# State space heads with outputs by channels, a first loop ordered by the scheduler, and an attention whose third and fourth queries are projected earlier

## The chip, the cores and the metric

The kernel runs on one core of a Trainium2 chip. The metric is the device time of one execution in microseconds (us); lower is better. Engines: TensorE (PE: matmuls, with weight loads in a queue of their own, PEld), VectorE (DVE), ScalarE (ACT), GpSimd (POOL), and SyncE (SP), which issues the DMAs of weights.

## The reference

One layer of a hybrid decoder on 256 tokens, D = 2048, in float32. Cut to what matters here:

```python
a = rmsnorm(h, attn_norm_g)
z, xBC, dt, q, k, v = split(a @ w_in)
x, B, C = silu(causal_conv4(xBC))              # x: 32 heads of 64; B, C: 4 groups of 128
# per group g (8 heads), chunks c of 128 tokens, acs = cumsum(dt * A):
y[l]  = sum_{s<=l} (C[l].B[s]) * exp(acs[l]-acs[s]) * dt[s]*x[s]      # own chunk
y[l] += exp(acs[l]) * C[l] @ prev_state                                # chunk before
y     = (y + d_skip * x) * silu(z)
y_ssm = rmsnorm_per_group(y) * ssm_norm_g
# attention: per-head norm of q and k, partial rope, window of 128, a sink per head
y_att = softmax_with_sink(q @ k.T) @ v
h = h + concat(y_ssm, y_att) @ w_out
h = h + w_down(silu(g) * u),  [g | u] = causal_conv3(rmsnorm(h) @ w_up)
h = h + sigmoid(rmsnorm(h) @ w_pg) * rmsnorm(p @ w_pe)
```

## The kernel before

The 256 tokens are two blocks b of 128. A float32 product is made of three matmuls: both factors are split into a high part in TensorE's fast float32 form and a low part (the rest), and hi·hi, hi·lo and lo·hi are added up in PSUM (lines 222 to 224 in `products`). A weight tile w is 128 x 2 x 512 (two k of 128 rows for 512 columns, 512 KB); it comes by DMA (line 207), ACT casts it to wh (line 192), DVE subtracts to wl (line 193), and it feeds 12 matmuls: 2 k, 2 blocks, 3 products. Pools: seven tiles w (`WR`), four each of wh and wl (`WB`), two pairs of accumulators acc, two tr tiles for transposes and two ms tiles in PSUM.

Stages in order, as far as the change goes:

*The first loop* (lines 340 to 379) projects the chunks B and C. Its weight tiles hold one k for the two chunks, so there are 16 tiles and two accumulator pairs, acc_b and acc_c. The order of PE's instructions is the code's (`manual_schedule`, line 339): per k first all six matmuls of chunk B, then those of C. Of the first three k each half of the tile is cast and subtracted by itself. Ahead stand 13 warm-up matmuls on constants (line 155). The dt products (lines 335 and 336) are spread over k = 11 to 13 and the end. Then `evac_scaled` (line 389) copies the accumulators to SBUF, ACT copies the dt sums to hsq (line 427), and chunks B and C are transposed and convolved (lines 299, 286, 288).

*The state space (SSD) stage* has four groups g; from here to the attention a scheduler orders the instructions of each engine. `ssd_x(g)` projects x (96 matmuls), loads the row differences seg from DRAM, makes the decays (seg, 128 x 8 x 128 per chunk, lines 484 to 497), convolves x and transposes it back to tokens (line 516); from that come the skip term yc (line 518) and Xd = dt·x (line 521). The heads: per chunk eight matmuls with seg as weights and Xd as moving data (64 columns, line 534), added to yc (line 535); for chunk 1 also the product with the state prev (line 538), scaled by exp(acs) on DVE (line 541) and added (line 542). So y has tokens on the partitions. `ssd_gate(g)` projects z (96 matmuls) and takes its Silu. `ssd_end` multiplies (line 557), sums squares on ACT, takes rstd (`rstd`, with a power on POOL, line 187), scales (line 561), transposes y on PE (line 272) and splits it (lines 195, 196) into the left factor of the output projection. Output 0 is projected here, outputs 1 to 7 (1 to 3 of the SSD, 4 to 7 of the attention) later.

*The attention* again has PE's order written by hand, in slots of 12 matmuls (2.7 us): keys 0 to 7, queries 0 8 to 15, values 16 to 23, queries 1 24 to 31, output 1 32 to 39, queries 2 40 to 47, output 2 48 to 55, queries 3 56 to 63, then outputs 3 to 7. A table `at` says ahead of which slot the scores (three pieces) and the value products of head pair j stand. Queries are normed and rotated, written as 16-bit halves by POOL (`half`), transposed by a DMA that SP issues in its order among the weight loads (line 688), and put together by POOL (line 689) to qT, for which the scores (line 738) wait. Scores go to DVE (s, line 742; nm, line 749), and the value products (line 779) run in pairs, with 64 weight columns each, into the two halves of the partitions. `add_to_h` (line 396) adds a projection to the residual h. Feed-forward and the rest are not touched.

Of the kernel before, what the change touches and what calls it, by code (L numbers as in the profile page):

```python
# [20 lines left out]
P = 128  # L21
# [44 lines left out]
def hybrid_layer(  # L66
# [87 lines left out]
    for _ in range(13):  # L154
        PE.matmul(ps, lhsT=one[:, :P], rhs=one, start=True, stop=True)
# [162 lines left out]
    with xin_:  # L318
        wd = sb(xin, [P, KT, 32], "wd")
        dhl = sb(xin, [P, KT, 64], "dhl", F32R)  # L320
        parts = {}

        def first_products(k, c):

            wh, wl = parts[k]
            acc = (acc_b, acc_c)[c]
            for part, wt in enumerate((wh, wh, wl)):
                for b in range(NB):
                    PE.matmul(acc[b], lhsT=aT(k, b)[part % 2], rhs=wt[:, c, :], start=(k == 0 and not part), stop=(k == KT - 1 and part == 2))

        dt_ps = ms_tile()

        def dt_products(k):
            hi, lo = aT.part(k)
            PE.matmul(dt_ps[:64, :T], lhsT=dhl[:, k, :], rhs=hi, start=(k == 0), stop=False, skip_group_check=True)
            PE.matmul(dt_ps[:32, :T], lhsT=dhl[:, k, :32], rhs=lo, start=False, stop=(k == KT - 1), skip_group_check=True)

        by_hand = ExitStack()
        by_hand.enter_context(tc.manual_schedule(engines={PE.engine}))
        for k in range(KT):  # L340
# [9 lines left out]
            n = 1 if k < 3 else KW  # L350
            for c in range(0, KW, n):
                split(w[:, c : c + n, :], wh[:, c : c + n, :], wl[:, c : c + n, :])
            parts[k] = wh, wl
            if k < KT - 2:
                for c in range(KW):
                    first_products(k, c)
            if k == 8:
                nc.sync.dma_start(wd, w_dt)
                nc.sync.dma_start(scw, ssm_cw)
                nc.sync.dma_start(rw, rows.partition_broadcast(P))  # L360
                nc.sync.dma_start(posi, pos)
                split(wd, dhl[:, :, :32], dhl[:, :, 32:])
# [5 lines left out]
            if k in (11, 12, 13):  # L368
                for i in range(4 * k - 44, 4 * k - 40):
                    dt_products(i)  # L370
        for c in range(KW):
            for k in (KT - 2, KT - 1):
                first_products(k, c)
        for k in range(KT - 4, KT):
            dt_products(k)
        by_hand.close()
        rx_ = rstd(ssx, D, NB, "rx_")
        V.tensor_copy(rx, rx_)

# [13 lines left out]
    def add_to_h(acc, n):  # L393
        for b in range(NB):
            hs = hres[b][:, n * NC : (n + 1) * NC]
            V.tensor_tensor(out=hs, in0=hs, in1=acc[b], op=ALU.add)  # L396
# [13 lines left out]
    def project(lhs, w, i0, ni, after=None):  # L410

        for n in range(4):
            acc = acc_pair()
            gemm(acc, lhs, [w[i, n] for i in range(i0 * KG // KW, (i0 + ni) * KG // KW)])
            add_to_h(acc, n)
# [5 lines left out]
    with tc.tile_pool(name="ssd", bufs=1) as sp, tc.tile_pool(name="dram", bufs=1, space=bass.MemoryType.DRAM) as dp:  # L421
        BT = sb(sp, [P, 4, T], "BT")
        CT = sb(sp, [P, 4, T], "CT")
        for c, (acc, dst, tag) in enumerate(((acc_b, BT, "ct"), (acc_c, CT, "Xd"))):
            t = evac_scaled(acc, sp, tag, 1)
            if c == 0:
                S.copy(dtT, dt_ps[:64, :T])
# [45 lines left out]
        eacs = sb(sp, [P, 64], "eacs")  # L473
        S.activation(out=eacs, in_=acs, func=AF.Exp)

        def ssd_x(g):
            segs = []
            for c in range(NB):
# [3 lines left out]
                if c == 0:  # L482
                    dec = sb(sp, [P, 8], "dec", bufs=2)
                    V.tensor_tensor(out=dec, in0=seg[:, :, P - 1], in1=acs[:, hs], op=ALU.subtract)
                    S.activation(out=dec, in_=dec, func=AF.Exp)
                V.tensor_tensor(out=seg, in0=seg, in1=bc(acs[:, hs], P), op=ALU.subtract)
# [25 lines left out]
            y, Xd = [], []  # L512
            for b in range(NB):
# [15 lines left out]
            for c in range(NB):  # L529
                yc = y[c]  # L530
                yp = ms_tile()
                for h in range(8):
                    hs = slice(h * HD, (h + 1) * HD)
                    PE.matmul(yp[:, hs], lhsT=segs[c][:, h, :], rhs=Xd[c][:, hs], start=True, stop=True)
                V.tensor_tensor(out=yc, in0=yc, in1=yp, op=ALU.add)
                if c:
                    off = ms_tile()
                    PE.matmul(off, lhsT=CT[:, g, c * P : (c + 1) * P], rhs=prev, start=True, stop=True)
                    t = sb(sp, [P, NC], "xe")
                    o = g * 16 + 8  # L540
                    V.tensor_tensor(out=v3(t, 8), in0=v3(off, 8), in1=bc(eacs[:, o : o + 8], HD), op=ALU.mult)
                    V.tensor_tensor(out=yc, in0=yc, in1=t, op=ALU.add)
# [11 lines left out]
        def ssd_end(g, y, zs):  # L554
            ssy = sb(sp, [P, NB], "ssy", bufs=2)
            for b in range(NB):
                V.tensor_tensor(out=y[b], in0=y[b], in1=zs[b], op=ALU.mult)
                S.activation(out=zs[b], in_=y[b], func=AF.Square, accum_out=ssy[:, b : b + 1])
            ry = rstd(ssy, NC, NB, "ry")
# [441 lines left out]
```

## Time and profile before

| | |
|---|---|
| Time, median of 3 runs | 1432.73 us (1432.59 to 1434.25) |
| The profiled execution | 1436.61 us, of which the span is 1434.9 us |
| Granted clock of TensorE | 1.00 |
| HBM | read 268.32 MB, written 2.13 MB |
| First loop | up to 55.11 us (the first transposes behind it) |
| SSD stage | about 55 to 316 us (last transposes of y at 315.33) |
| Scores of the attention, first wait for qT | 371.95 us |

Durations of single instructions come from the profiled execution; they are read against its span, not against the median. A matmul row shows the time from issue to its modelled end, so that neighbours overlap: the distance of two starts is what one costs. In the timeline and the groups below, "x16" counts instructions, and a plain float32 product shows as two.

### The profile page before, as it was taken

How to read it: one execution, taken by the hardware profiler on the slowest of the kernel's cores; microseconds unless marked ns; L12 is line 12 of the kernel's file. 1: busy time of each engine (PE TensorE's matmuls, PEld its weight loads, DVE VectorE, ACT ScalarE, POOL GpSimd, SP SyncE). 2: the span in 40 equal slices, each digit the busy share in tenths (PEclk: the TensorE clock that was granted, in tenths of full speed). 3: DMA queues.
4: the chain of work that ended last, by engine and by line, in shares of the span. 5: the costliest groups of instructions: out<-in, count | busy, mean ns of one | idle time of the engine just before them, and what ended most of it. 6: DMA issues, size and time to landing. Idle time of an engine off the chain costs nothing.

```text
span 1434.9 us, 18092 instructions
## 1 busy us (share of the span) xinstructions
PE 1423.2 (99%) x6527; PEld 1167.3 (81%) x6527; DVE 984.1 (69%) x1242; ACT 804.2 (56%) x1101; POOL 286.2 (20%) x212
## 2 busy tenths in 40 slices
PE   9999999999999999999999999999999999999998
PEld 7887888888787778888888888888888888888887
DVE  6678876776678897656667646765675576476854
ACT  6675555644567666556556446545554554455643
POOL 0002010008345432013243112201320131120000
PEclk9999999999999999999999999999999999999999
DMA  9656656548687778577887767867876877776671
GB/s 332 236 173 198 215 177 185 171 148 223 188 220 187 209 220 220 168 211 207 219 226 202 217 205 206 225 196 198 230 208 192 223 201 218 206 208 190 208 226 65
DMA packets 163467, 292.62 MB, mean 204 GB/s; under 512 B 93041, under 2 KB 95921, under 8 KB 162993
## 3 DMA queue, kind: packets, MB, share of 16 engines
q1 hardware_dynamic: 162944, 290.99, 70.5%
q8 instruction: 51, 0.84, 0.2%
q10 hardware_dynamic: 432, 0.48, 0.1%
q14 instruction: 40, 0.32, 0.1%
HBM read 268.32 MB, written 2.13 MB: 188 GB/s over the span
## 4 chain that ended last, share of the span: by engine, by line
PE 68%; DVE 1%; ACT 0%; issue 0%; POOL 0%; DVEq 0%; ACTq 0%
PE acc L222 22%; PE acc L224 22%; PE acc L223 22%; PE tr L779 1%; PE tr L272 0%; PE sc L738 0%; DVE wl L193 0%; ACT s L753 0%; DVE nm L749 0%; DVE s L742 0%; ACT wh L192 0%; DVE sg L931 0%; ACT s L761 0%; DVE qkr L672 0%; DVE h L396 0%
## 5 line engine op out<-in xcount | busy, mean ns | idle before, releaser
L193 DVE TENSOR_TENSOR wl<-w,wh 128x1024 fp32r<-128x1024 f32 (+1 forms) x495 | 634.9, 1288 | 378.5 <-ACT wh L192 376.4
L192 ACT CAST wh<-w 128x1024 fp32r<-128x1024 f32 (+1 forms) x495 | 514.8, 1045 | 480.7 <-PE acc L224 431.4
L223 PE MATMUL acc<-wl,ah 128*128 128x512 f32 x1278 | 500.1, 391 | 1.5 <-DVE wl L193 1.5
L224 PE MATMUL acc<-wh,al 128*128 128x512 f32 x1278 | 499.0, 391 | 0.0
L222 PE MATMUL acc<-wh,ah 128*128 128x512 f32 x1278 | 498.3, 392 | 0.0
L223 PEld LDWEIGHTS acc<-wl,ah 128*128 128x128 f32 x1278 | 240.1, 188 | 52.3 <-DVE wl L193 2.4
L222 PEld LDWEIGHTS acc<-wh,ah 128*128 128x128 f32 x1278 | 240.1, 188 | 51.0 <-issue 1.4
L224 PEld LDWEIGHTS acc<-wh,al 128*128 128x128 f32 x1278 | 240.1, 188 | 50.1 <-issue 0.7
L224 PE MATMUL acc<-wh,gl 128*128 128x512 f32 x352 | 137.1, 390 | 0.0
L223 PE MATMUL acc<-wl,gh 128*128 128x512 f32 x352 | 137.1, 390 | 0.0
L222 PE MATMUL acc<-wh,gh 128*128 128x512 f32 x352 | 136.5, 390 | 0.0
L881 POOL COPY half<-u 128x1024 uint16<-128x1024 uint16 x44 | 62.0, 1422 | 264.3 <-ACT u L879 264.3
L222 PE MATMUL acc<-wh,yh 128*128 128x512 f32 x256 | 101.6, 397 | 0.6 <-DVE h L396 0.6
L223 PE MATMUL acc<-wl,yh 128*128 128x512 f32 x256 | 99.9, 390 | 0.0
L224 PE MATMUL acc<-wh,yl 128*128 128x512 f32 x256 | 99.7, 390 | 0.0
L884 POOL COPY uc<-flip 128x1024 uint16<-128x1024 uint16 x44 | 54.9, 1248 | 177.2 <-DMA flip<-half 174.9
L223 PEld LDWEIGHTS acc<-wl,gh 128*128 128x128 f32 x352 | 66.1, 188 | 13.7
L224 PEld LDWEIGHTS acc<-wh,gl 128*128 128x128 f32 x352 | 66.1, 188 | 13.6
L222 PEld LDWEIGHTS acc<-wh,gh 128*128 128x128 f32 x352 | 66.1, 188 | 13.6
L288 DVE SCALAR_TENSOR_TENSOR cv<-uc,fcw,cv 128x254 f32<-128x254 f32 (+1 forms) x176 | 73.2, 476 | 3.4 <-ACT cv L286 3.4
L396 DVE TENSOR_TENSOR h<-h,acc 128x512 f32<-128x512 f32 x112 | 73.0, 678 | 1.8 <-PE acc L224 1.8
L222 PEld LDWEIGHTS acc<-wh,yh 128*128 128x128 f32 x256 | 48.1, 188 | 14.6 <-issue 2.0
(239 smaller groups left out, 1129.2 us busy)
## 6 DMA issues: line engine op xcount, KB each, us to landing
w<-in_w_up_dram SPq DMA_DIRECT2D x176, 512.0 KB, 4.2
w<-in_w_in_dram SPq DMA_DIRECT2D x126, 512.0 KB, 4.2
w<-in_w_down_dram SPq DMA_DIRECT2D x88, 512.0 KB, 4.3
w<-in_w_out_dram SPq DMA_DIRECT2D x64, 512.0 KB, 4.2
w<-in_w_pg_dram SPq DMA_DIRECT2D x32, 512.0 KB, 4.3
seg<-scr SPq DMA_DIRECT2D x8, 512.0 KB, 5.0
xt<-in_xT_dram SPq DMA_DIRECT2D x16, 128.0 KB, 7.0
h<-in_x_dram SPq DMA_DIRECT2D x2, 1024.0 KB, 8.7
```

Of the source, the lines that this page charges most:

```text
L192: S.copy(hi, src)
L193: V.tensor_tensor(out=lo, in0=src, in1=hi.bitcast(F32), op=ALU.subtract)
L222: PE.matmul(acc[b], lhsT=hi, rhs=wh[:, i, :], start=(k == 0), stop=False)
L223: PE.matmul(acc[b], lhsT=hi, rhs=wl[:, i, :], start=False, stop=False)
L224: PE.matmul(acc[b], lhsT=lo, rhs=wh[:, i, :], start=False, stop=(k == total - 1 or (b == NB - 1 and k + 1 == whole)))
L288: V.scalar_tensor_tensor(out=dst[:, s:], in0=ps[:, : T - s], scalar=taps[n - 1 - s], in1=dst[:, s:], op0=ALU.mult, op1=ALU.add)
L396: V.tensor_tensor(out=hs, in0=hs, in1=acc[b], op=ALU.add)
L779: PE.matmul(v3(o[e * HD : (e + 1) * HD, kv * 2 * P : (kv + 1) * 2 * P], 2), lhsT=v[kb][:, vs], rhs=pT[e][:, :, kb, :], start=(kb == 0), st ...
L881: G.tensor_copy(half.rearrange("p (a n) -> p a n", a=2), u_.bitcast(U16).rearrange("p (n a) -> p a n", a=2))
L884: G.tensor_copy(uc[:, :, b * P : (b + 1) * P].bitcast(U16).rearrange("p f (t a) -> p f t a", a=2), flip.rearrange("p (a f) t -> p f t a", ...
```

## The change

1. **First loop.** Eight warm-up matmuls instead of 13. PE's order is the scheduler's. Only k = 0 is split in halves. The small loads for dt come after k = 3 instead of 8. The dt products use one ms tile after the loop in the code, and ACT's copy of them stands directly behind.
2. **SSD heads.** y has channels on the partitions, 128 x 4 x 256. The state term goes into the same accumulation: a tile grown = exp(acs)·C for chunk 1, made by ACT and DVE, is the moving factor and prev the weight. Two heads write the two halves of the partitions. The skip is added while y is read from PSUM. z is brought to channels by POOL copies (16-bit halves), a DMA transpose that SP issues, and POOL copies back (zT), as the queries are. The split reads y directly, with no transpose on PE. The squares are summed over channels by a reduction and two matmuls with a column of ones, and rstd is applied when the output projection is added to h.
3. **Attention.** Order: queries 1, queries 2, output 1, queries 3, output 2, outputs 3 to 7. The table of scores and values is shifted.

```diff
-    for _ in range(13):
+    for _ in range(8):
         PE.matmul(ps, lhsT=one[:, :P], rhs=one, start=True, stop=True)
...
-        by_hand.enter_context(tc.manual_schedule(engines={PE.engine}))
...
-            n = 1 if k < 3 else KW
-            for c in range(0, KW, n):
-                split(w[:, c : c + n, :], wh[:, c : c + n, :], wl[:, c : c + n, :])
-            parts[k] = wh, wl
-            if k < KT - 2:
-                for c in range(KW):
-                    first_products(k, c)
-            if k == 8:
+            for c in range(0, KW, 1 if k == 0 else KW):
+                cs = slice(c, c + 1 if k == 0 else KW)
+                split(w[:, cs, :], wh[:, cs, :], wl[:, cs, :])
+            for c, acc in enumerate((acc_b, acc_c)):
+                for b in range(NB):
+                    h, l = aT(k, b)
+                    PE.matmul(acc[b], lhsT=h, rhs=wh[:, c, :], start=(k == 0), stop=False)
+                    PE.matmul(acc[b], lhsT=h, rhs=wl[:, c, :], start=False, stop=False)
+                    PE.matmul(acc[b], lhsT=l, rhs=wh[:, c, :], start=False, stop=(k == KT - 1))
+            if k == 3:
...
+        S.copy(dtT, ps[:64, :T])
...
-    def add_to_h(acc, n):
+    def add_to_h(acc, n, scale=None):
...
+                V.scalar_tensor_tensor(out=hs, in0=acc[b], scalar=scale[:, b : b + 1], in1=hs, op0=ALU.mult, op1=ALU.add)
...
+                else:
+                    grown = sb(sp, [P, 8, P], "grown")
+                    S.activation(out=grown, in_=seg, func=AF.Exp)
+                    V.tensor_tensor(
+                        out=grown, in0=grown, in1=CT[:, g, P:].unsqueeze(1).to_broadcast([P, 8, P]), op=ALU.mult
+                    )
...
-                yc = sb(sp, [P, NC], f"yc{b}", bufs=2)
-                V.tensor_tensor(out=v3(yc, 8), in0=v3(tr, 8), in1=bc(dsk[:, g * 8 : (g + 1) * 8], HD), op=ALU.mult)
-                y.append(yc)
...
-                    PE.matmul(yp[:, hs], lhsT=segs[c][:, h, :], rhs=Xd[c][:, hs], start=True, stop=True)
-                V.tensor_tensor(out=yc, in0=yc, in1=yp, op=ALU.add)
-                if c:
-                    off = ms_tile()
-                    PE.matmul(off, lhsT=CT[:, g, c * P : (c + 1) * P], rhs=prev, start=True, stop=True)
...
+                own = [(0, i, Xd[0], segs[0]) for i in range(2)]
+                for i in range(2):
+                    own += [(1, i, Xd[1], segs[1]), (1, i, prev, grown)]
+                for c, i, left, right in own:
+                    for e_ in range(2):
+                        h = 4 * half + 2 * i + e_
+                        PE.matmul(
+                            yp[e_ * HD : (e_ + 1) * HD, i, c * P : (c + 1) * P],
+                            lhsT=left[:, h * HD : (h + 1) * HD],
+                            rhs=right[:, h, :],
...
+                    V.scalar_tensor_tensor(
+                        out=y[:, f, :], in0=xc[:, f, :], scalar=skip[:, 4 * g + f : 4 * g + f + 1], in1=yp[:, i, :], op0=ALU.mult, op1=ALU.add
+                    )
...
+                half = sb(sp, [P, 2 * NC], ("xe", "prev")[b], U16)
+                G.tensor_copy(half.rearrange("p (a n) -> p a n", a=2), zs[b].bitcast(U16).rearrange("p (n a) -> p a n", a=2))
+                flip = sb(sp, [P, 8, P], f"Xd{b}", U16)
+                nc.sync.dma_start_transpose(flip, half)
+                G.tensor_copy(
+                    zT[:, :, b * P : (b + 1) * P].bitcast(U16).rearrange("p f (t a) -> p f t a", a=2),
...
+            V.tensor_tensor(out=y, in0=y, in1=zT, op=ALU.mult)
...
+            S.activation(out=sq, in_=y, func=AF.Square)
+            s1 = sb(sp, [P, T], "ysum")
+            V.tensor_reduce(out=s1, in_=sq.rearrange("p f t -> p t f"), axis=AX.X, op=ALU.add)
+            ps = ms_tile()
             for b in range(NB):
-                V.tensor_scalar_mul(y[b], y[b], ry[:, b : b + 1])
-            yT = Lhs(yp_, KG, "y")
-            transpose_split(y, yT, 0, g_ssm[:, 4 * g : 4 * g + 4])
-            return (yT, w_out, g, 1)
+                PE.matmul(ps[:, b : b + 1], lhsT=s1[:, b * P : (b + 1) * P], rhs=ones, start=True, stop=True)
+            return yT, w_out, g, 1, rstd(ps[:, :NB], NC, NB, f"ry{g}")
...
-        for j, first, value in ((0, (28, 31, 34), 48), (1, (43, 46, 50), 64), (2, (58, 61, 65), 79), (3, (75, 77, 80), 93)):
+        for j, first, value in ((0, (29, 32, 35), 49), (1, (44, 47, 51), 65), (2, (58, 61, 66), 79), (3, (73, 75, 80), 93)):
...
                 lambda: q(1),
+                lambda: q(2),
                 lambda: output(1),
-                lambda: q(2),
-                lambda: output(2),
                 lambda: q(3),
-                *(lambda i=i: output(i) for i in range(3, 8)),
+                *(lambda i=i: output(i) for i in range(2, 8)),
```

How the instructions stand now, at three places. First PE's row at the start of the first loop, before: acc_29 and acc_30 are the two blocks of chunk B, acc_31 and acc_32 those of chunk C; ah and al are the high and low part of the activations.

```order
L155 MATMUL ms_103<-const-bfloat16-1.0 128x512
L329 MATMUL acc_29_152<-wh_163,ah_18_141 128x512
L329 MATMUL acc_30_153<-wh_163,ah_18_141 128x512
L329 MATMUL acc_29_152<-wh_163,al_19_142 128x512
L329 MATMUL acc_30_153<-wh_163,al_19_142 128x512
L329 MATMUL acc_29_152<-wl_164,ah_18_141 128x512
L329 MATMUL acc_30_153<-wl_164,ah_18_141 128x512
L329 MATMUL acc_31_154<-wh_163,ah_18_141 128x512
L329 MATMUL acc_32_155<-wh_163,ah_18_141 128x512
```

The same place in the changed kernel:

```order
L155 MATMUL ms_103<-const-bfloat16-1.0 128x512
L337 MATMUL acc_29_147<-wh_155,ah_18_136 128x512
L337 MATMUL acc_30_148<-wh_155,ah_18_136 128x512
L337 MATMUL acc_31_149<-wh_155,ah_18_136 128x512
L337 MATMUL acc_32_150<-wh_155,ah_18_136 128x512
L338 MATMUL acc_29_147<-wl_156,ah_18_136 128x512
L339 MATMUL acc_29_147<-wh_155,al_19_137 128x512
L338 MATMUL acc_30_148<-wl_156,ah_18_136 128x512
L339 MATMUL acc_30_148<-wh_155,al_19_137 128x512
```

Chunk C's products with wh have moved ahead of all products with wl and with the low activations of chunk B.

Second, PE's row at the heads of chunk 1 in the last group, before; the matmuls around them are those of the key projection, which already runs:

```order
L223 MATMUL acc_523_2674<-wl_2768,ah_22_145 128x512
L224 MATMUL acc_523_2674<-wh_2767,al_23_146 128x512
L534 MATMUL ms_2433<-Xd_463_2415,seg_2205 128x64 x8
L538 MATMUL ms_2443<-prev_2421,CT_568 128x512
L222 MATMUL acc_524_2675<-wh_2767,ah_22_145 128x512
```

And in the changed kernel, the end of one half of the heads and the other half (xN counts products; ms is the PSUM tile):

```order
L223 MATMUL acc_531_2687<-wl_2763,ah_22_140 128x512
L531 MATMUL ms_2430<-grown_2214,prev_2427 64x128 x2
L531 MATMUL ms_2430<-seg_2212,Xd_468_2421 64x128 x2
L531 MATMUL ms_2430<-grown_2214,prev_2427 64x128 x2
L531 MATMUL ms_2445<-seg_2202,Xd_466_2414 64x128 x4
L531 MATMUL ms_2445<-seg_2212,Xd_468_2421 64x128 x2
L531 MATMUL ms_2445<-grown_2214,prev_2427 64x128 x2
L531 MATMUL ms_2445<-seg_2212,Xd_468_2421 64x128 x2
L531 MATMUL ms_2445<-grown_2214,prev_2427 64x128 x2
L224 MATMUL acc_531_2687<-wh_2762,al_23_141 128x512
```

The weights are now Xd and prev with 64 columns, the moving data seg and grown with 128; the off product stands among the heads, in pairs, and there is no scaling behind it.

Third, DVE's row at the last scores of the third head pair (j = 2) in the attention, before:

```order
L742 TENSOR_TENSOR s_817_3989<-sc_3990,band_125 128x1024
L193 TENSOR_TENSOR wl_4082<-w_4080,wh_4081 128x1024
L396 TENSOR_TENSOR h_1_83<-h_1_83,acc_812_3969 128x512
L749 TENSOR_REDUCE nm_3996<-s_817_3989 128x4
L396 TENSOR_TENSOR h_2_84<-h_2_84,acc_813_3970 128x512
L193 TENSOR_TENSOR wl_4100<-w_4098,wh_4099 128x1024
```

And in the changed kernel, where line 383 is the addition to h with a scale:

```order
L193 TENSOR_TENSOR wl_4559<-w_4557,wh_4558 128x1024
L756 TENSOR_TENSOR s_928_4466<-sc_4467,band_120 128x1024
L383 SCALAR_TENSOR_TENSOR h_1_83<-acc_923_4446,ry_513_2640,h_1_83 128x512
L763 TENSOR_REDUCE nm_4473<-s_928_4466 128x4
L383 SCALAR_TENSOR_TENSOR h_2_84<-acc_924_4447,ry_513_2640,h_2_84 128x512
L764 TENSOR_TENSOR nm_4473<-nm_4473,nsink_2665 128x4
L193 TENSOR_TENSOR wl_4577<-w_4575,wh_4576 128x1024
```

The weight split that stood between the scores and the first addition to h now stands ahead of the scores.

More of the change, by code (lines that the diff above doesn't have):

```diff
@@ L320, in hybrid_layer @@
         dhl = sb(xin, [P, KT, 64], "dhl", F32R)
[L321 to L338, printed above, removed]
-        by_hand.enter_context(tc.manual_schedule(engines={PE.engine}))
         for k in range(KT):
@@ L800, in output @@
         def output(i):
[L801 removed]
+            lhs, w, i0, ni, scale = held.pop(i)
             for n in range(4):
```

77 lines of the change are left out of this document (41 added, 36 removed).

## The prediction

> **What bounds the kernel now.** I read the busy times and the chain of waits of the page first, then TensorE's (PE's) waits up to the end of the attention, then the timeline at the places that the diff touches.
>
> ```profile
> PE 1423.2 (99%) x6527; PEld 1167.3 (81%) x6527; DVE 984.1 (69%) x1242; ACT 804.2 (56%) x1101; POOL 286.2 (20%) x212
> PE 68%; DVE 1%; ACT 0%; issue 0%; POOL 0%; DVEq 0%; ACTq 0%
> ```
> ```profile
> PE sc L738 <- POOL qT L689: 2.6, 2, 1.4
> PE acc L223 <- DVE wl L193: 1.5, 2, 1.0
> PE tr L299 <- issue: 0.9, 1, 0.9
> PE ms L155 <- PEq L991: 0.8, 1, 0.8
> PE acc L222 <- DVE h L396: 0.6, 1, 0.6
> ```
>
> PE is busy for 1423.2 of 1434.9 us and stands almost alone in the chain. In the stretch that the diff touches (0 to 640 us) it waits 6.4 us in all, 5.6 of them behind the start. So a gain is either PE work taken out or one of these waits. The profiled execution took 1436.61 us for a span of 1434.9; the median of the three runs is 1432.73. All terms are differences in one span, and I take their sum off the median.
>
> **Term A, the first loop: +1.4 us.**
>
> ```profile
> 0.84 5.71 PE L155 MATMUL ms<-const-bfloat16-1.0 128*128 128x512 bf16 x13 [0.84 <-PEq L991]
> 5.99 1.22 PE L329 MATMUL acc<-wh,ah 128*128 128x512 f32 x2
> 7.04 0.62 PE L329 MATMUL acc<-wh,al 128*128 128x512 f32 x2
> 7.50 0.62 PE L329 MATMUL acc<-wl,ah 128*128 128x512 f32 x2
> ...
> 34.27 0.61 PE L329 MATMUL acc<-wh,al 128*128 128x512 f32 x2
> ...
> 55.11 0.41 PE L299 MATMUL tr<-ident,ct 128*128 128x128 f32 x2 [0.88 <-issue]
> ```
> ```profile
> 4.05 0.62 ACT L192 CAST wh<-w 128x512 fp32r<-128x512 f32 x1 [1.32 <-DMA w<-in_w_in_dram]
> 5.61 0.62 ACT L192 CAST wh<-w 128x512 fp32r<-128x512 f32 x1 [0.94 <-DMA w<-in_w_in_dram]
> 7.67 1.31 ACT L192 CAST wh<-w 128x512 fp32r<-128x512 f32 x2 [0.66 <-DMA w<-in_w_in_dram]
> 11.91 1.05 ACT L192 CAST wh<-w 128x1024 fp32r<-128x1024 f32 x1
> 54.32 1.26 ACT L389 ACTIVATE ct<-acc,rx 128x512 f32<-128x512 f32 x2 [0.35 <-PE ms L336]
> 55.48 0.35 ACT L427 COPY hsq<-ms 64x256 f32<-64x256 f32 x1
> ```
> ```profile
> 13.00 1.23 DVE L193 TENSOR_TENSOR wl<-w,wh 128x1024 fp32r<-128x1024 f32 x1 [0.40 <-ACT wh L192]
> ```
>
> From 7.50 to 34.27 us stand 118 matmuls: 0.227 us each, with no slack, so a delay at the start is never caught up. A warm-up matmul takes 5.71 / 13 = 0.44 us; eight end at 0.84 + 3.5 = 4.35 instead of 6.55. The first product needs the first half of wh (4.05 + 0.62 = 4.67), and its third matmul now needs the second half (5.61 + 0.62 = 6.23), since wh·ah of both column chunks comes first. PE thus has two short gaps, and its first product ends no later for it. In before the first real pair cost 1.05 us and all after it 0.45: matmuls became fast at about 7.04, after 6.2 us of unbroken work.
>
> The second k, k = 1, is no longer split in halves: one cast of 1.05 starts when both halves have landed (the second half's cast stands about 7.67 + 0.66 = 8.33), wh is there at 9.4, wl 1.23 later at 10.6. Four wh·ah matmuls may run before; eight wait for wl: 10.6 + 8 x 0.227 = 12.4. In before the 24 matmuls of k = 0 and 1 end at 5.99 + 1.05 + 22 x 0.227 = 12.0. So +0.4 is the lower end. If the gaps keep matmuls at 0.52 us until some 10.5 us, k = 0 ends there, and k = 1's 12 end at 10.5 + 12 x 0.227 = 13.2: +1.2. If it takes another 6.2 unbroken us from 6.23 on, they stay slow to 12.4 and k = 1 ends near 14.8: +2.8. I take +1.1, because the first products' row lies in before right behind unbroken work and here behind gaps.
>
> By the Trainium skill, page "TensorE: Matmul & The Clock Gate", section "What's actually happening", the array starts at half clock and gets full clock after a busy window of some 3.4 us, by a window that runs freely. Eight warm-up matmuls fill 3.5 us; by that rule the clock could be up at 4.35 and the term would be its lower end, +0.4; the trace shows 0.52 us per matmul still at 5.99, after 5.2 us of work, so I do not count on it.
>
> At the end of the loop ACT copies the dt sums (0.35 us) ahead of the two ct evacuations, on which the first transposes (0.88 us of idle PE at 55.11) wait: +0.3. The rest moved in the loop (loads of w_dt and rows five steps sooner, dt products spread by the scheduler) is the same work; that PE keeps its 0.227 there is cover enough, nothing counted. Term A: 1.1 + 0.3 = **+1.4**, from +0.4 to +3.1.
>
> **Term B, PE work of the SSD heads: -6.3 us.**
>
> ```profile
> 298.13 1.89 PE L534 MATMUL ms<-Xd,seg 128*128 128x64 f32 x16
> 300.15 0.39 PE L222 MATMUL acc<-wh,ah 128*128 128x512 f32 x1
> ...
> 302.23 1.89 PE L534 MATMUL ms<-Xd,seg 128*128 128x64 f32 x16
> ...
> 305.11 0.40 PE L223 MATMUL acc<-wl,ah 128*128 128x512 f32 x1
> ...
> 315.33 1.03 PE L272 MATMUL tr<-ident,yc 128*128 128x128 f32 x8
> 316.43 0.39 PE L224 MATMUL acc<-wh,al 128*128 128x512 f32 x1
> ```
> ```profile
> 485.69 2.81 PE L779 MATMUL tr<-s,v 128*64 128x256 f32 x24
> 488.77 0.40 PE L223 MATMUL acc<-wl,yh 128*128 128x512 f32 x1
> ```
> ```profile
> L779 PEld LDWEIGHTS tr<-s,v 128*64 128x64 f32 x96 | 6.6, 137 | 4.3 <-issue 1.4
> ```
>
> In each of these blocks one projection matmul stands as well, 0.227 us. Block 0's heads: 300.15 - 298.13 - 0.227 = 1.79. Block 1's with the off product: 305.11 - 302.23 - 0.227 = 2.65. The eight transposes of y: 316.43 - 315.33 - 0.227 = 0.87. Together 5.31 us a group. The head instructions, of 64 columns, take 1.79 / 16 = 0.112 each, as their 128-column weight load does.
>
> The changed group has 24 logical products, 48 instructions (each plain f32 product shows as two, as above), with 64 weight columns and 128 moving ones, in pairs that write the two halves of the partitions. The nearest row is the attention's values: 24 instructions of the same 128*64 form and 256 columns took 488.77 - 485.69 - 0.227 = 2.85 in 12 pairs; their pitch within the block is 0.217, which leaves 0.25 of switching. So the two of a pair run side by side. At half the columns a pair is 0.11; 24 x 0.11 = 2.64, and two blocks a group with 0.33 each to switch: 3.30. The two ones matmuls for the norm are four 128-column loads, 4 x 0.11 = 0.44. 3.74 - 5.31 = -1.57 a group, four groups: **-6.3**. Without the switching it is -8.9. If nothing ran side by side: 48 x 0.106 + 0.2 + 0.44 = 5.74, +0.43 a group, +1.7.
>
> Here a rule speaks against it: the same page, section "The mechanism", says a weight load overlaps a running matmul only where its row group differs, and both of a pair use all 128 rows; by it the sum would be that of rival 1. The row disagrees: L779's loads of 137 ns, two a pair, are 0.27 us and would not fit in its 0.217 beside the matmuls unless they overlapped.
>
> **Term C, the waits around the heads: 0.**
>
> ```profile
> L535 DVE TENSOR_TENSOR yc<-yc,ms 128x512 f32<-128x512 f32 x8 | 5.5, 682 | 4.2 <-PE ms L534 4.2
> ```
> ```profile
> 112.37 2.12 DVE L193 TENSOR_TENSOR wl<-w,wh 128x1024 fp32r<-128x1024 f32 x1
> 133.31 1.23 DVE L486 TENSOR_TENSOR seg<-seg,acs 128x1024 f32<-128x1024 f32 x1 [4.76 <-DMA seg<-scr]
> ```
> ```profile
> L884 POOL COPY uc<-flip 128x1024 uint16<-128x1024 uint16 x44 | 54.9, 1248 | 177.2 <-DMA flip<-half 174.9
> L881 POOL COPY half<-u 128x1024 uint16<-128x1024 uint16 x44 | 62.0, 1422 | 264.3 <-ACT u L879 264.3
> ```
> ```profile
> DMA to landing us min/median/max: 4.2/5.1/7.2
> ```
>
> DVE drops eight operations of 512 elements a group (L518, L535, L541, L542, L557) at 0.68, 5.4 us. It gains three of 1024 elements (grown, the gate multiply, the reduction) at 1.23 as in the seg row, 3.7. Two scalings by the norm go and four skips of 256 elements come, at an estimated half of 0.68 each a net 0.7. That is 1.0 less. The 1.5 us of PE waits for wl come from DVE held by seg, whose load is unchanged (133.31). Against it POOL gets four copies a group, 2 x 1.42 + 2 x 1.25 = 5.3 us, and a wl beside POOL work can take 2.12 instead of 1.22 (112.37, where POOL runs the affine select). A gain of the whole 1.5, or a loss of one such delay a group that nothing covers, 4 x 0.9 = 3.6, are the ends; between them I take nothing, since the load falls while the seg rows, where the waits start, stay. The gate's path (half copies 2.84, transposing DMA 5.1, copies 2.5, multiply 1.2) takes 11.6 us; in the changed order the multiply stands at least 80 matmuls, 18 us, behind the last head, with a wl right behind it. That hides it.
>
> **Term D, the attention: -2.2 us.**
>
> ```profile
> 475.03 1.15 POOL L689 COPY qT<-flip 128x1024 uint16<-128x1024 uint16 x1 [14.51 <-PE acc L224]
> ```
> ```profile
> 469.08 5.55 SPq L688 DMA_TRANSPOSE flip<-half  x2
> ```
> ```profile
> 450.23 1.21 DVE L749 TENSOR_REDUCE nm<-s 128x4 f32<-128x1024 f32 x1
> ```
>
> Both waits for qT (1.4 and 2.6 - 1.4 = 1.2) should go. The first queries' scores come one slot (12 x 0.227 = 2.72 us) later. The second wait came because a half lay on SP (below, rival 2); the third and fourth queries are now projected eight slots (21.8 us) sooner, while their scores move by at most two. That is -2.6, and -2.9 with the refill of PE behind the two waits (an estimate of 0.15 each). The h wait of 0.6 goes too or returns: at the third queries' last scores DVE has now wl, s, h, nm, h, wl in a row, with nm (1.21) ahead of the second h, more work in a row than a slot of 2.72 holds (wl 1.23 and s 1.2 stand ahead of the first h). I put +0.4 to +1.6 for it, +0.7 as the nearest to the 0.6 seen. Sum: -2.9 + 0.7 = **-2.2**, from -3.7 (all waits gone) to +0.5.
>
> **Sum.** 1.4 - 6.3 + 0 - 2.2 = -7.1: 1432.7 - 7.1 = 1425.6, say **1425.5 us**.
>
> **Rivals.**
> 1. *Pairs don't run side by side.* B becomes +1.7, the sum +0.9: 1433.6. For it: a pair's loads share the rows; against it the 0.217 of L779. Chance 0.06.
> 2. *The gate comes late (slower).* SP issues the flip behind the weight loads, which wait for free buffers: in before a half done at 460.5 (14.51 before 475.03) was issued at 469.08, 8.5 us later. With that in front the gate's path is 11.6 + 8.5 = 20.1 us against a cover of 18; a second flip behind it adds about 1: 3 us a group with wl behind the multiply, +12, so 1437.6. It decides once the half waits longer than 6 us on SP. Against it: the SSD's flips meet no softmax transposes on SP. Chance 0.07.
> 3. *New waits for wl.* POOL's copies slow two wl's a group by 0.9 and DVE has no idle there: with 1.4 us a group, +5.6, near 1431. Chance 0.12.
> 4. *The queries' move does nothing.* Another transpose is late instead, D = 0: 1427.7. Chance 0.10.
>
> **How the numbers follow.** Forecast 0.65. 0.2%, 2.9 us, is about what a measurement of this kernel can tell from no change: faster is below 1429.9, slower above 1435.6. Faster takes 0.62 of the forecast's 0.65, rival 4 (0.10) and a part of rival 3 (0.05): 0.77. Slower is rival 2 (0.07), and 0.01 for ends that add up. The rest is same: 0.15. The range goes from the sum with B and D towards their better ends together (1420) past rival 3 to just short of rival 1 (1433); outside lie rivals 1 and 2 and rare sums.
>
> **What would show it.** A: the first conv transpose near 56.5 instead of 55.11. B: the heads' rows (64 wide, line 531 of the changed kernel) at about 0.11 a pair, no transposes of y, PE busy some 6 us less. C: no PE wait on wl longer than before's; DVE idle before the gate's multiply with POOL's zT as releaser, and PE waiting after it, would be rival 2. D: no wait of L738's successor for qT. The prediction is wrong if pairs show 0.2 us, or if PE's waits up to 640 us add up to more than 8.

## The result, and the profile after

The changed kernel takes 1446.07 us (median of 4 runs, 1442.86 to 1447.27), the kernel before in the same comparison 1433.49 (1432.59 to 1434.69): a ratio of 1.0083, 95% interval 1.007 to 1.0097. It is 12.6 us slower where 7.1 us less were forecast. The profiled execution of the changed kernel is its shortest run (1442.86), while that of the kernel before, 1436.61, was 3.1 us longer than the median; so the two traces are 6.2 us apart, not 12.6, and what the three longer runs lost beyond the profiled one is in no trace.

The page of the changed kernel, busy times, and then the first rows of its chain of waits:

```profile
PE 1419.6 (99%) x6562; PEld 1158.3 (80%) x6562; DVE 990.7 (69%) x1230; ACT 804.6 (56%) x1089; POOL 309.7 (21%) x228
PE 64%; DVE 1%; ACT 0%; issue 0%; DVEq 0%
```

PE is busy for 3.6 us less, and the span is 6.2 us longer: work went, and more waiting came. PE's waits over the changed kernel's whole span (us in total, times, longest):

```profile
PE sc L752 <- POOL qT L703: 6.9, 1, 6.9
PE acc L222 <- DVE h L383: 3.8, 4, 1.3
PE acc L223 <- DVE wl L193: 1.5, 2, 1.2
PE acc L337 <- ACT wh L192: 1.2, 2, 1.0
PE tr L299 <- ACT ct L372: 1.1, 1, 1.1
PE ms L155 <- PEq L1004: 0.8, 1, 0.8
PE tr L512 <- ACT xc L507: 0.5, 1, 0.5
```

One wait of 6.9 us for qT stands where before had two of 2.6 together, and it is at the scores that were to wait no more. Both programs run equally many projection matmuls behind the first loop, so the start of the one with the same number in both timelines shows where the time went. A slot's scores stand directly behind its 12 matmuls: those of slot 28 in the kernel before start at 371.95.

| Projection matmul, by its number | before | changed | difference |
|---|---|---|---|
| first one behind the first loop | 55.27 | 56.34 | +1.07 |
| first of slot 28 of the attention | 367.70 | 363.16 | -4.54 |
| first of slot 32 | 382.51 | 384.34 | +1.83 |
| first of slot 64 | 482.87 | 485.42 | +2.55 |
| one of slot 86 | 555.05 | 561.26 | +6.21 |
| last of the program | 1429.37 | 1435.60 | +6.23 |

So from the first loop to slot 28, which is mostly the SSD stage, the changed kernel gains 5.6 us in these two traces; between slots 28 and 32 it loses 6.4 and in the rest of the attention another 4.4; behind that nothing changes. By slot 32 the kernel before has run one piece of scores more, of 1.1 us, so the late first scores cost 7.5 us and the rest of the attention 3.3. PE's timeline of the changed kernel at the 6.4 us, then its windows of 10 us (busy time of each engine, then PE's granted clock, DMA share, GB/s):

```profile
375.66 2.08 PE L752 MATMUL sc<-kT,qT 64*128 64x128 f32 x16 [6.90 <-POOL qT L703]
377.67 0.79 PE L222 MATMUL acc<-wh,ah 128*128 128x512 f32 x1
378.26 0.63 PE L223 MATMUL acc<-wl,ah 128*128 128x512 f32 x1
...
379.97 0.44 PE L224 MATMUL acc<-wh,al 128*128 128x512 f32 x1
```
```profile
370.00:380.00 10.00, 4.34 (x22) 3.63 (x23) 3.29 (x3) 1.15 (x1) 2.30 (x2) 0.66 0.73 151
```

The scores take 2.0 us instead of 1.1, and the matmuls behind them stand 0.43 apart instead of 0.23: the clock fell during the idle (to 0.50 from 373.24 to 380.06), which cost another 2 us here. Why qT came so late is in the rows of POOL (half and qT) and of SP (weight loads and the flip between them), changed kernel:

```profile
358.42 1.38 POOL L715 COPY half<-qkr 128x1024 uint16<-128x1024 uint16 x1
...
374.46 1.15 POOL L703 COPY qT<-flip 128x1024 uint16<-128x1024 uint16 x1 [10.07 <-DMA flip<-half]
```
```profile
351.63 17.12 SPq L207 DMA_DIRECT2D w<-in_w_in_dram  x8
368.80 1.24 SPq L702 DMA_TRANSPOSE flip<-half  x1
```

And SP of the kernel before:

```profile
353.92 11.21 SPq L207 DMA_DIRECT2D w<-in_w_out_dram  x5
365.19 1.24 SPq L688 DMA_TRANSPOSE flip<-half  x1
```

The half is ready at 359.8, but the flip (the transposing DMA) leaves at 368.8. Counted over the traces, SP has issued 109 weight tiles (line 207) ahead of this flip in the kernel before and 112 in the changed one: the scheduler, which orders SP, has put the flip behind three more loads. Each load waits for a free buffer, which PE frees at one slot of 2.7 us. The changed kernel's 109th load went out at 361.24; had the flip stood behind it, as before, qT would have been there 6.9 us later, at 368.1, and PE asks for it at 368.76. Three loads more and one slot more for the scores: 1.4 + 3 x 2.7 - 2.7 = 6.8 us, and 6.9 were measured.

### The profile page after: what moved, and what is told of

It is laid out like the page before. It is cut to its first block, busy times and chain, and to the rows that moved or that the text cites. A ratio compares the mean times of both kernels' runs of the same rounds, so it can differ in the third digit from the quotient of the medians.

```text
span 1441.1 us, 18180 instructions
## 1 busy us (share of the span) xinstructions
PE 1419.6 (99%) x6562; PEld 1158.3 (80%) x6562; DVE 990.7 (69%) x1230; ACT 804.6 (56%) x1089; POOL 309.7 (21%) x228
## 4 chain that ended last, share of the span: by engine, by line
PE 64%; DVE 1%; ACT 0%; issue 0%; DVEq 0%
PE acc L222 21%; PE acc L223 21%; PE acc L224 21%; PE tr L272 0%; PE tr L793 0%; PE sc L752 0%; DVE wl L193 0%; DVE den L771 0%; ACT wh L192 0%; DVE sg L944 0%; ACT s L767 0%; DVE h L383 0%; DVE s L756 0%; DVE nm L763 0%; DVE sg L945 0%
## 5 line engine op out<-in xcount | busy, mean ns | idle before, releaser
L223 PEld LDWEIGHTS acc<-wl,yh 128*128 128x128 f32 x256 | 48.1, 188 | 11.4 <-DVE wl L193 1.7
```

The costliest lines, as they stand in the source:

```text
L223: PE.matmul(acc[b], lhsT=hi, rhs=wl[:, i, :], start=False, stop=False)
```

## The experiments

Each time stands beside that of the kernel before, measured next to it: medians in us, with the 95% interval of their ratio.

### Each part alone

The three parts of the diff were put into the kernel before one at a time.

> Only part 1 (first loop, warm-up) put into the kernel before. Theory (each part costs what its stretch shows in the changed kernel's profile): the first transposes come 1.1 us later, SP's order in the attention stays as before, so 1434.6 us, +1.1. Rival (the late flip comes from the loop's change): the first queries' scores wait about 7 us for qT and the time goes above 1440.

> Only part 2 (SSD heads by channels) put into the kernel before; the attention's order and slots are those of before. Theory (the heads' change moves the first queries' transposing DMA behind three more weight loads on SP, while their scores stay in slot 28): SSD stage -5.6 us as in the changed kernel, the wait of the first scores for qT 9.5 us (6.9 + 2.7 for the one slot sooner) instead of 1.4, and 2 us or more of matmuls at a lower clock behind it: 1437 to 1443 us. Rival (the late flip comes from the attention's new order): the wait stays 1.4 us and the time is 1427 to 1429.

> Only part 3 (order of queries and outputs, slots of scores and values) put into the kernel before. Theory: flips keep their places on SP, the first scores wait 0 for qT (one slot later), the third queries' wait of 1.2 us goes, new waits for h and wl of 2 to 5 us come: 1432 to 1436 us. Rival (the new order itself makes the first queries late): a wait of about 7 us for qT and 1440 us or more.

Measured against 1434.22: part 1 1436.43 (1.0005 to 1.0023), part 2 1443.74 (1.0048 to 1.0078), part 3 1437.87 (1.0014 to 1.0033). Part 1 cost 2.2 where 1.1 was expected, and part 2 came out just above its 1437 to 1443. The heads' change alone brings the late first qT, though not a line of the attention is touched. PE's timeline of part 2 alone:

```profile
378.93 2.08 PE L771 MATMUL sc<-kT,qT 64*128 64x128 f32 x16 [9.88 <-POOL qT L722]
```

The wait is 9.88 (9.5 expected), one slot more than in the changed kernel, since the scores stand one slot sooner. The order of SP agrees: with part 2 the flip stands behind three more loads with or without parts 1 and 3, and in the kernels without part 2 it stays where it was. The other half of the expectation failed: slot 28 comes 1.5 us sooner than in the kernel before, not 5.6. Behind the first transposes the SSD stage has PE waits of 3.7 us, where before had 1.5. Part 3 alone is worse than the 1432 to 1436 expected. Its profile has no wait for qT, but waits of 3.6 us for qkr, of which this is the longest (its trace is its shortest run but one):

```profile
411.03 0.50 PE L222 MATMUL acc<-wh,yh 128*128 128x512 f32 x1 [2.74 <-ACT qkr L665]
```

Queries 2 now follow queries 1 directly; output 1 needs their accumulators, and ACT, busy with the softmax of the first pair, empties them 2.7 us late.

### The first scores later

```diff
-        for j, first, value in ((0, (29, 32, 35), 49), ...
+        for j, first, value in ((0, (30, 32, 35), 49), ...    # one slot later
+        for j, first, value in ((0, (32, 34, 36), 49), ...    # three slots later
```

> The changed kernel with the first queries' first scores one slot later (30 instead of 29), the next two as they are. Theory (the flip leaves SP at a fixed place among the weight loads, so each slot of 2.7 us takes as much off the wait): the wait for qT is 6.9 - 2.7 = 4.2 us, and the time 2.7 us down and up to 3 more if the clock holds: 1440.5 to 1443.5 us. Rival (the flip moves along with the scores): the wait stays near 7 us and the time at 1446.

> The changed kernel with the first queries' scores three slots later (32, 34, 36 instead of 29, 32, 35). Theory (the flip leaves SP when slot 28 has ended plus 2.8 us and qT is there 6.9 us behind it; the idle lowers the clock): no wait for qT at the first scores, no stretch at a lower clock, time down by 9 to 12 us: 1433 to 1437 us, with a spread over runs like that of before. Rival (the time lost is somewhere else, the wait only takes up slack that a later wait would take): less than 4 us faster than the changed kernel.

One slot later: 1440.52 against 1434.32 (1.0031 to 1.0059). Three slots later: 1434.09 against 1434.22 (0.9988 to 1.0007). PE's timeline with one slot:

```profile
375.46 2.08 PE L752 MATMUL sc<-kT,qT 64*128 64x128 f32 x16 [4.35 <-POOL qT L703]
...
381.05 0.53 PE L224 MATMUL acc<-wh,al 128*128 128x512 f32 x1
```

and PE's waits with three slots, up to 700 us:

```profile
PE acc L223 <- DVE wl L193: 2.2, 4, 0.9
...
PE acc L222 <- ACT qkr L679: 0.9, 1, 0.9
...
PE acc L222 <- DVE h L383: 0.6, 1, 0.6
```

The waits for qT at slots 28 (part 2 alone), 29, 30 and 32 are 9.9, 6.9, 4.4 and none: about 2.7 us a slot, as it must be for a flip at a fixed place among the loads. With one slot the time fell by 5.5 us, as if the clock had held, but it did not (the row at 381.05); the 2.9 us beyond the slot are not explained by this trace. Without the wait the kernel is 12 us faster, and level with the kernel before.

### Another queue, and PE kept busy

```diff
-            nc.sync.dma_start_transpose(flip, ...)
+            nc.scalar.dma_start_transpose(flip, ...)          # act_queue
```
```diff
+            if j == 0 and b == 0:                             # warm_wait, ahead of the scores
+                for _ in range(24):
+                    PE.matmul(sc[:, 0]..., lhsT=one[:, :P], rhs=one, start=True, stop=True)
```

> The changed kernel with the attention's transposing DMAs issued by ScalarE instead of SP, so that no weight load stands in front of them. Theory (the first qT is late because its flip stands behind 112 weight loads in SP's queue): the first scores wait less than 2 us for qT, no stretch at a lower clock, 1434 to 1440 us; ScalarE now stands still where a half isn't ready. Rival (the flip is late because its data or the DMA engines are): the wait for qT stays above 5 us and the time above 1443.

> The changed kernel with 24 more bf16 matmuls on constants (5.4 us) ahead of the first queries' scores, written into the scores' own PSUM tile, so that PE is busy through most of the wait. Theory (part of the loss is the lower clock behind 6.9 us of idle, more of it in the runs of 1446 than in the profiled one): the scores start when they did, no matmul behind them is slow, 1440 to 1443 us. Rival (the clock costs nothing, the spread has another source): 1445 to 1448 us.

On ACT's queue: 1445.15 against 1434.14 (1.006 to 1.0087), no gain; the expectation that the wait goes once the flip leaves SP's queue fell. ACT's rows there, POOL's row that makes the half, and the wait:

```profile
368.70 1.04 ACT L192 CAST wh<-w 128x1024 fp32r<-128x1024 f32 x1 [1.66 <-PE acc L224]
368.77 4.51 ACTq L702 DMA_TRANSPOSE flip<-half  x2
```
```profile
364.60 1.92 POOL L715 COPY half<-qkr 128x1024 uint16<-128x1024 uint16 x1
```
```profile
376.05 1.23 PE L752 MATMUL sc<-kT,qT 64*128 64x128 f32 x8 [7.38 <-POOL qT L703]
```

The scheduler put the flip behind casts, and each of these waits for PE just as the loads do; it left at 368.77, as on SP. But here the half itself was ready only at 366.5, 6.7 us later than in the changed kernel, so that at most 2.3 of the 7.38 us come from the flip's place on ACT. This run therefore can't separate the queue from the data. In the changed kernel the half is ready 9.0 us ahead of its flip, so there the data are not what is late.

With PE kept busy: 1443.45 against 1434.14 (1.0048 to 1.0079), just above the range expected, and 9.3 us above before instead of 12.6. The scores came 7.2 us late as ever, but ran at full clock:

```profile
369.98 5.42 PE L750 MATMUL sc<-const-bfloat16-1.0 128*128 128x512 bf16 x24
377.22 1.16 PE L755 MATMUL sc<-kT,qT 64*128 64x128 f32 x16 [1.81 <-POOL qT L703]
378.31 0.50 PE L222 MATMUL acc<-wh,ah 128*128 128x512 f32 x1
```

The lower clock thus costs some 3 us of the 12.6 (2 in the profiled execution), as far as one more replanned kernel can show it: its trace waits longer than the changed kernel's for h and qkr. The 12 us between the changed kernel and the one with scores three slots later are 8.4 in their two traces, where PE's waits (15.8 against 8.9 in all up to 700 us) and the 2 of clock cover them. The rest belongs to the three runs of the changed kernel that are 3.0 to 4.4 us longer than the profiled one. Their granted clock over the whole span was 0.993 to 0.996 against its 0.997, so more time at the lower clock is a candidate, which is not shown.

### Parts 1 and 2 without part 3

The table of before was kept, but for `(0, (32, 34, 36), 49)`.

> Part 2 alone (SSD heads by channels) in the kernel before, with the first queries' scores in slots 32, 34, 36 and their values in 49, all else of before. Theory (the heads' change gains 5.6 to 6.3 us in its own stage, and all that it lost in the run of part 2 alone, 9.5 us net, is the late first qT with the lower clock behind it): 1427 to 1430 us, clearly faster than before. Rival (the gain of the SSD stage is taken up again by later waits of the attention, whatever the slots): 1432 us or more.

> The same with part 1 (first loop, warm-up) as well. Theory (part 1 costs 1 to 2 us and does nothing else): 1 to 2 us above the run of part 2 with late scores, 1428.5 to 1432 us. Rival (part 1's loss is hidden by what follows): the same time within 0.5 us.

Part 2 with late scores: 1430.54 against 1434.14 (0.9969 to 0.9987), just above the range expected. With part 1 as well: **1428.61** (0.9948 to 0.9973), the fastest kernel of the study, 5.5 us below the kernel before; PE waits for nothing between 380 and 640 us. So the heads' gain is real and reaches the end. Part 1, expected to cost 1 to 2 us, gains 1.9 here and cost 2.2 alone. In the trace of the run without part 1 the first loop ends 1.7 us sooner, yet slot 0 of the attention starts 1.5 us later: the scheduler laid out the SSD stage otherwise. PE's waits there, behind the first transposes:

```profile
PE tr L299 <- ACT ct L389: 1.8, 1, 1.8
PE ms L595 <- DVE ysum L592: 0.9, 1, 0.9
PE acc L223 <- DVE wl L193: 0.8, 2, 0.7
```

With the smaller ones they are 3.7 us against 1.9 with part 1, and behind those for ysum and wl the granted clock is 0.50 from 156.9 to 160.4, some 1.5 us more; together that is about the 3.2 us by which this stretch is longer. The run of part 2 alone shows the same waits and the same fall of the clock. So the stretch from the first transposes to slot 28 became 4.3 to 5.9 us shorter than before's 312.6 only in the traces that have both parts and the pairs; with part 2 but not part 1 it is 1.3 and 2.0 shorter, and the kernels without part 2 differ by more among themselves (311.0 to 313.8). Effects of some 3 us hang on each replanning, and part 1 by itself can't be told from them.

### What part 3 costs

On the 1428.61 kernel: the changed table with the old order, or the changed order with the old table; the run of three slots later has both.

> Parts 1 and 2 with the first scores late as in the run of 1428.6 us, the old order of queries and outputs, but the changed table for the other scores and values. Theory (what part 3 costs comes from its order, with queries 2 directly behind queries 1 and ScalarE busy with softmax when their accumulators must be emptied): 1428 to 1430.5 us. Rival (it comes from the table, scores that collide with the additions to h on VectorE): 1432 us or more.

> Parts 1 and 2 with the first scores late, the changed order of queries and outputs, but the old table for the other scores and values. Theory (the order costs): 1432.5 to 1435.5 us, with PE waiting for ScalarE's qkr or for h. Rival (the table costs): 1428 to 1430.5 us.

The table alone takes 1434.51 against 1434.32 (0.9992 to 1.001), the order alone 1438.76 (1.0019 to 1.0039), both together 1434.09. The first came out where its rival stood and the second above its range, and with them fell the split into one that costs and one that doesn't: each costs without the other. With the table alone the fourth queries' scores come at slot 73 with the queries still projected late; with the order alone h comes late (the two rows, one of each kernel):

```profile
517.04 1.93 PE L752 MATMUL sc<-kT,qT 64*128 64x256 f32 x8 [2.89 <-POOL qT L703]
```
```profile
501.91 0.47 PE L222 MATMUL acc<-wh,yh 128*128 128x512 f32 x1 [2.38 <-DVE h L383]
```

Together they still cost 5.5 us (1434.09 to 1428.61). Of these, 3.6 show as PE waits between 380 and 640 us (1.9 for wl, 0.9 for qkr, 0.8 for wh), where the kernel of 1428.61 has none; the rest is in no single wait.

### The pairs

The heads' products in another order, so that neighbours use the same half of the array's columns.

```diff
-                for c, i, left, right in own:
-                    for e_ in range(2):
+                for e_ in range(2):
+                    for c, i, left, right in own:
```

> Parts 1 and 2 with the first scores late, and the heads' products in another order: all of the lower half of the partitions, then all of the upper, so that neighbours use the same weight columns. Theory (two halves run side by side): each product costs about 0.11 us an instruction instead of 0.055, 48 x 0.11 - 24 x 0.11 = 2.6 us a group, 10 us in all: 1437 to 1440 us. Rival (loads bound a pair, nothing runs side by side): 1428 to 1430 us.

1438.92 against 1434.32 (1.0022 to 1.005), 10.3 us above the paired kernel. The groups of PE in the SSD stage, unpaired, then paired (1428.61):

```profile
L531 PE MATMUL ms<-seg,Xd 128*64 128x128 f32 x128 | 15.5, 279 | 0.0
L531 PE MATMUL ms<-grown,prev 128*64 128x128 f32 x64 | 12.4, 276 | 0.0
```
```profile
L531 PE MATMUL ms<-seg,Xd 128*64 128x128 f32 x128 | 9.9, 276 | 0.0
L531 PE MATMUL ms<-grown,prev 128*64 128x128 f32 x64 | 6.4, 279 | 0.0
```

27.9 us against 16.3, so the halves do run side by side. But these busy times hold overlaps; by starts a group of 48 takes 1.5 us more, 5.8 us in four groups. In the unpaired trace neighbours stand 0.109 us apart, which in the paired one is the distance of two pairs; only where one half follows the other do some four of each still run side by side, hence 1.5 instead of 2.6. The rest of the 10.3 goes at least in part to new waits: with this order the flip moved once more, behind another load, and PE waits 2.7 us for qT in two pieces. The size hit the forecast partly by chance.

## Why the prediction was wrong

*Term A, the first loop (+1.4).* Right in size. In the four traces with the loop of before the first transposes start at 54.50 to 55.11 us, in the ten traces with the new loop at 55.58 to 56.93: 1.4 apart in the mean, and 1.07 in the changed kernel's own. (The lower end of +0.4 left out the term's own +0.3.) How long matmuls stay slow differs between executions of the same loop. In the changed kernel they were fast soon, although PE had idled 0.2 and 1.0 us; these are the last products of k = 0 with wh, and the first behind them:

```profile
6.37 0.73 PE L337 MATMUL acc<-wh,ah 128*128 128x512 f32 x2 [1.02 <-ACT wh L192]
6.94 0.40 PE L338 MATMUL acc<-wl,ah 128*128 128x512 f32 x1
7.17 0.39 PE L339 MATMUL acc<-wh,al 128*128 128x512 f32 x1
```

From 6.94 on they stand 0.23 apart, and k = 1 ended 0.3 late, near the lower end. In the run of part 1 alone, whose first loop is the same, they stand 0.43 apart until 9.4:

```profile
8.10 0.63 PE L338 MATMUL acc<-wl,ah 128*128 128x512 f32 x1
8.52 0.63 PE L339 MATMUL acc<-wh,al 128*128 128x512 f32 x1
...
9.90 0.39 PE L339 MATMUL acc<-wh,al 128*128 128x512 f32 x1
```

And in the trace of 1428.61 the granted clock is 1.00 from 3.8 us, 0.50 from 7.2 and 1.00 again from 10.6, behind gaps of 0.4 and 1.3 us. So "they stay slow until some 10.5 us" is true of some executions and not of others. Before's fast matmuls began at 7.04, after 13 warm-up matmuls; in the other traces with 13 at 5.4 to 6.8. Whole runs can't settle this term.

*Term B, the heads (-6.3).* Right. The last group in the changed kernel, PE's timeline:

```profile
291.82 0.88 PE L531 MATMUL ms<-seg,Xd 128*64 128x128 f32 x12
...
296.94 0.44 PE L531 MATMUL ms<-grown,prev 128*64 128x128 f32 x4
...
299.05 0.50 PE L224 MATMUL acc<-wh,al 128*128 128x512 f32 x1
```

The larger block takes 299.05 - 296.94 = 2.11 us for 18 pairs, 0.117 a pair; with the smaller one (0.81) and the switching around both the group takes 3.2; 3.3 was forecast. The stretch up to slot 28 came to -5.6 in these traces, and to as much only where part 1 stood beside it (above). Rival 1 fell; the unpaired run shows it too, where a single instruction costs the 0.109 us of a pair. By the rule on weight loads, which the prediction took from the Trainium skill, page "TensorE: Matmul & The Clock Gate", section "The mechanism", a load would not overlap a running matmul of the same rows; the traces disagree for the 64-column halves, with 0.117 us a pair.

*Term C, the waits around the heads (0).* Right in sum for the changed kernel: PE waited 1.6 us in the SSD stage behind its first transposes (wl 0.3, h 0.8, xc 0.5) where it had waited 1.5. Two of its readings were off: the reduction over channels took 2.0 us, not 1.23, and the gate's multiply stood 51 to 77 projection matmuls behind the last head, not 80. Rival 2 did not come: zT was ready 1.5 to 5.0 us ahead of each multiply. Its mechanism, though, a transposing DMA held by SP behind weight loads, is the one that decided the case, at another place. And in both runs of part 2 without part 1 PE waits 0.9 us for the reduction (ysum) that follows the gate's multiply.

*Term D, the attention (-2.2).* Here it failed: +10.8 in the traces. The step that failed is "Both waits for qT (1.4 and 2.6 - 1.4 = 1.2) should go"; for the first it rested on "The first queries' scores come one slot (12 x 0.227 = 2.72 us) later". I counted the slot that the scores got and took the flip to stay where it was on SP; it had moved three loads back, and the wait of 1.4 us became one of 6.9. SP's order in the changed kernel could have been read beforehand, like that of PE and DVE, and gives 6.8 us. The clock behind so long an idle, 2 to 3 us, was in no rival. Rival 4 ("Another transpose is late instead") came nearest, but counted nothing lost for it. PE's waits up to 640 us add up to 15.8, above the 8 that was to show the prediction wrong. The second half of the step held: the wait of 1.2 for the third queries went. The last piece, +0.7 for h, was mis-sized. DVE's rows of the changed kernel where three h waits of 0.92, 0.76 and 1.34 us stand:

```profile
505.09 1.22 DVE L756 TENSOR_TENSOR s<-sc,band 128x1024 f32<-128x1024 f32 x1
506.22 0.74 DVE L383 SCALAR_TENSOR_TENSOR h<-acc,ry,h 128x512 f32<-128x512 f32 x1
506.88 1.21 DVE L763 TENSOR_REDUCE nm<-s 128x4 f32<-128x1024 f32 x1
508.01 0.74 DVE L383 SCALAR_TENSOR_TENSOR h<-acc,ry,h 128x512 f32<-128x512 f32 x1
...
513.05 2.10 DVE L771 TENSOR_TENSOR den<-den,es 128x4 f32<-128x4 f32 x1
515.07 0.74 DVE L383 SCALAR_TENSOR_TENSOR h<-acc,ry,h 128x512 f32<-128x512 f32 x1
```

The first two are the collision that the prediction read from the order (s ahead of one h, nm ahead of the other); the third was not foreseen (below). Part 3 as a whole costs 3.6 us alone and 5.5 on top of parts 1 and 2. Its order and its table each cost without the other, which leaves open what the new order could do with a table fitted to it.

*The base.* The waits of before that term D was to win back, 2.6 us for qT among them, stood in a run 3.1 us longer than the median; a typical run may have less to give (in the trace of part 1 alone they are 1.1).

*What stays open.* Which operation of part 2 moves the flip in the scheduler's plan was not tried, nor a flip put back by hand; the evidence for its place is the dependence on the slot, the count of loads, and the order with and without part 2.

## What to carry to other kernels

Where a scheduler lays out the queues, a change in one stage can move a transfer in another that no line of the diff touches: compare the place of every DMA on the chain that feeds a hand-placed consumer, counted in loads and slots, before trusting that its wait stays. A consumer at a fixed slot needs a margin of its transfer's whole latency behind the last PE-paced load ahead of it. And an idle of several microseconds on TensorE costs more than itself: 6.9 us of it cost another 2 to 3 here. Read such effects from more than one trace: the same first loop ran with different clocks, and the stretch with the heads gained 5.6 us beside part 1 and 1.5 without it.

## What the runs showed of the hardware

- The granted clock in the records is 1.00 or 0.50, and once up it stays in each state for 3.41 us or a multiple: 0.50 for 3.41 us (table alone, from 517.24), 6.83 (changed kernel, from 373.24) and 10.24 (part 2 alone, from 372.59). It fell behind single idles of PE of 1.81 us (unpaired), 2.38 (order alone), 2.89 (table alone) and more, up to 9.88, and behind two of 0.91 and 0.69 close together (both runs of part 2 without part 1). It did not fall behind the 2.74 us of part 3 alone. Counted in stretches of 3.41 us from a change of the clock in the same trace, each of the 13 stretches that end in a fall holds at least 1.47 us of idle, while the 2.74 us lie across two stretches, with 1.44 and 1.30. The largest idle in a stretch without a fall behind it is 1.75 us, so the limit is not sharp in this reckoning. How long the clock stays low does not follow the idle alone: matmuls were slow for 4.4 us behind 6.9 of idle and for 5.9 behind 4.35. The Trainium skill, page "TensorE: Matmul & The Clock Gate", section "What's actually happening", has half clock after an idle window of some 3.4 us, which runs freely; the steps of 3.41 us agree, but here windows idle for less than half were enough.
- A DVE operation on four elements a partition (513.05 above) took 2.10 us, where most of its kind take 0.15 to 0.2, and ended with a POOL copy beside it:

```profile
512.95 2.18 POOL L703 COPY s<-flip 128x2048 uint16<-128x2048 uint16 x1 [5.69 <-ACT wh L192]
```

It delayed an addition to h and PE by 1.34 us. This agrees with the Trainium skill, page "SBUF — State Buffer", section "SBUF: two separate sides", by which a DVE operation with two SBUF inputs and a GpSimd operation that reads SBUF lock each other out for a whole instruction.
